# Attention scores from one 512-column product, its two halves added on the way out of PSUM

## The chip, the cores and the metric

The kernel runs on one core of a Trainium2 chip. The metric is the device time of one execution in microseconds (us). TensorE (PE in the profile) multiplies matrices, VectorE (DVE) and ScalarE (ACT) work elementwise, GpSimd (POOL) here issues DMAs and clears memory, SyncE (SP) issues most weight loads from HBM.

## The reference

A trunk of 4 layers over 256 tokens of width 2048, with 256 memory tokens. Layers 0 and 3 use multi-head latent attention (16 heads), layer 1 sparse attention (32 heads, the top 64 keys of a query), layer 2 sliding-window attention (32 heads, with sinks). Every layer also attends to the memory with 4 heads of width 256, gates, projects out and adds to the residual:

```
s = (einsum(qn, k_nope) + einsum(qr, k_rope)) * scale      # latent
s = einsum(qb, kg) * 64**-0.5 + bias                       # sparse, window
s = einsum(mq, mk) * 256**-0.5                             # memory
p = softmax(where(mask, s, -1e30));  o = p @ v
y = concat([self_out, mem_out]) * silu(gate);  x = x + y @ w_out[i]
```

All arithmetic is fp32.

## The kernel before

To get near fp32 precision from TensorE's faster fp32r format, the kernel keeps an operand as two fp32r parts: an exact part and a remainder (`split`, lines 67 to 69: ScalarE copies and rounds, L60, VectorE subtracts, L69). A product of two such operands is three products: exact by exact, exact by remainder, remainder by exact. All big projections are made so: `rows_by` (L265 to L267, three products of 512 columns for each 128 features) and `columns_by` (L285, one product whose 512 moving columns are the exact part and the remainder side by side, and L289, one of 256 columns). In `columns_by` the two halves of a PSUM bank hold two partial sums, which are added when the bank is read out (`total`, `head_parts`).

Weights come from HBM into a ring of 5 tiles `wr`; `parts_of` splits each 128x512 piece into `wh` and `wl` (rings of 3). So TensorE is fed by one L60 and one L69 for every 1536 columns or so.

The layers' work is split into six parts (two of memory heads, four of self heads). Each part has a projection, an attention and an output projection `w_out`. The instructions of all of them are put in order by the framework's planner, which simulates the engines with modelled durations; so a part's attention is threaded between the next part's projection products on TensorE. Each engine then executes its queue strictly in the planned order.

The scores of a head are made for two blocks of 128 queries, b = 0 and b = 1, in `score(b)`. Block 0 sees 128 keys, block 1 sees 256. In block 0 the keys' exact part and remainder (128 columns each) already are the moving columns of one 256-column product, and `masked_softmax` adds the second half with the bias (L527) before the fused add-and-minimum (L529, a `tensor_tensor_reduce`, followed by a read of its accumulator). In block 1, exact part and remainder are two products of 256 columns into the same 256 columns of PSUM, so L529 needs no addition before it. The memory heads (`memory_attend`, L577) make six products of 256 columns for each block, take the maximum (L588) and the exponential (L592) straight from PSUM. In the sparse layer the bias of a block is first added to the selection (`bs`, L962).

Small work tiles of these steps rotate through tags: `e` (4 buffers: `u`, `bs`, `e`, `th`), `mp` (4 PSUM banks).

Of the kernel before, what the change touches and what calls it, by code (L numbers as in the profile page):

```python
# [8 lines left out]
F32 = mybir.dt.float32  # L9
F32R = mybir.dt.float32r  # L10
I32 = mybir.dt.int32
AF = mybir.ActivationFunctionType
OP = mybir.AluOpType
AX = mybir.AxisListType

P = 128
S = 256
# [4 lines left out]
BIG = 3e38  # L22
# [9 lines left out]
def kernel(ctx: ExitStack, tc: tile.TileContext, a: dict, out: bass.AP,  # L32
                             kinds=(0, 1, 2, 0)):
    nc = tc.nc
# [4 lines left out]
    wk = ctx.enter_context(tc.tile_pool(name="wk", bufs=1))  # L39
# [9 lines left out]
    def small(name, n, dt=F32, bufs=None):  # L49
        return wk.tile([P, n], dt, name=name, tag=f"s{n}" if bufs is None else name,  # L50
                       bufs=bufs or 6)
# [7 lines left out]
    def copy_act(o, i, scale=1.0):  # L59
        inst = nc.scalar.activation(o, i, AF.Copy, scale=scale)  # L60
        if pinned:
            tc.keep_in_program_order(inst)
# [245 lines left out]
    class Norm:  # L308
# [37 lines left out]
        def finish(self):  # L346
            s2 = small("xs2", 2)
            nc.vector.tensor_reduce(s2, self.ss.rearrange("p (t c) -> p t c", t=2), AX.X, OP.add)
            self.rstd = small("xr", 2, bufs=3)
            rsqrt_mean(self.rstd, s2, D)  # L350
            self.eighth = small("x8", 2, bufs=3)
            nc.vector.tensor_scalar(self.eighth, self.rstd, 0.125, None, op0=OP.mult)
            half = small("xh", 2)
            nc.vector.tensor_scalar(half, self.rstd, 0.5, None, op0=OP.mult)
            self.half = wk.tile([P, S], F32, name="half", tag="half", bufs=1)
            spread(self.half, half)
# [158 lines left out]
    def masked_softmax(score, bias, scale=None, nsk=None):  # L515

        es = []
        mn, sm = small("mn", 2), small("sm", 2)  # L520
        for b in range(2):
            n = (b + 1) * P
            sp = score(b)
            u = wk.tile([P, S], F32, name="u", tag="e", bufs=4)
            bi = bias(b, n)
            if b == 0:
                nc.vector.tensor_add(u[:, :n], sp[:, n:2 * n], bi)  # L527
                bi = u[:, :n]
            nc.vector.tensor_tensor_reduce(u[:, :n], sp[:, :n], bi, -1.0,  # L529
                                           nsk if nsk is not None else BIG,  # L530
                                           op0=OP.add, op1=OP.min, accum_out=mn[:, b:b + 1])
            e = wk.tile([P, S], F32, name="e", tag="e", bufs=4) if nsk is None else u
            if scale is None:
                nc.scalar.activation(e[:, :n], u[:, :n], AF.Exp, bias=mn[:, b:b + 1], scale=-1.0,
                                     accum_out=sm[:, b:b + 1])
            else:
                ms = small("ms", 2)
                nc.vector.tensor_mul(ms[:, :1], mn[:, b:b + 1], scale[0][:, b:b + 1])
                nc.scalar.activation(e[:, :n], u[:, :n], AF.Exp, bias=ms[:, :1],
                                     scale=scale[1][:, b:b + 1], accum_out=sm[:, b:b + 1])  # L540
            es.append(e)
        r = small("rc", 2)
        if nsk is not None:
            d = small("sd", 2)
            nc.vector.tensor_scalar(d, mn, nsk, None, op0=OP.subtract)
            e2 = small("se", 2)
            nc.scalar.activation(e2, d, AF.Exp)
            s3 = small("sa", 2)
            nc.vector.tensor_add(s3, sm, e2)
            nc.vector.reciprocal(r, s3)  # L550
        else:
            nc.vector.reciprocal(r, sm)
        for b in range(2):
            normalized(es[b], r[:, b:b + 1], (b + 1) * P)
        return weights_T(es, [(0, 0), (1, 0), (1, 1)])
# [20 lines left out]
    def memory_attend(nm, kT, v, qT, gT):  # L576
        y = act.tile([P, 2, 4, S], F32R, name="y", tag="y", bufs=2)  # L577
        for h in range(2):
            es = []
            mn, sm = small("mn", 2), small("sm", 2)  # L580
            for b in range(2):
                sp = misc("msp")
                qs = slice(b * P, (b + 1) * P)
                seq = [(qT[h][:, u, k, qs], kT[h][:, v_, k, :])
                       for k in range(2) for u, v_ in ((0, 0), (0, 1), (1, 0))]
                for n_, (l, r_) in enumerate(seq):
                    nc.tensor.matmul(sp[:, :S], l, r_, start=n_ == 0, stop=n_ == len(seq) - 1)
                nc.vector.tensor_reduce(mn[:, b:b + 1], sp[:, :S], AX.X, OP.max, negate=True)  # L588
                ms = small("ms", 2)
                nc.vector.tensor_mul(ms[:, :1], mn[:, b:b + 1], nm.col("rstd", b))  # L590
                e = wk.tile([P, S], F32, name="e", tag="e", bufs=4)
                nc.scalar.activation(e, sp[:, :S], AF.Exp, bias=ms[:, :1], scale=nm.col("rstd", b),  # L592
                                     accum_out=sm[:, b:b + 1])
                es.append(e)
            r = small("rc", 2)
            nc.vector.reciprocal(r, sm)
            for b in range(2):
                normalized(es[b], r[:, b:b + 1], S)
            tp = weights_T(es, [(0, 0), (1, 0), (0, 1), (1, 1)])
            pH, pL = (wk.tile([P, 768], F32R, name="pT", tag="pT", bufs=PT)[:, :512] for z in range(2))  # L600
            split(pH, pL, tp)
            o = misc("mo")
            for j in range(2):
                c = (2 * h + j) * P
                seq = [(v[z][:, t, c:c + P], p_[:, t * S:(t + 1) * S])
                       for t in range(2) for z, p_ in ((0, pH), (0, pL), (1, pH))]
                for n_, (l, r_) in enumerate(seq):
                    nc.tensor.matmul(o[:, j * S:(j + 1) * S], l, r_, start=n_ == 0, stop=n_ == 5)
            gated(y, o, gT, 2 * h)
        return y  # L610
# [13 lines left out]
    class Latent:  # L624
# [102 lines left out]
        def attend(self, qn, qr, kn, v, gT):  # L727
            y = act.tile([P, 2, 4, S], F32R, name="y", tag="y", bufs=2)
            for h in range(4):
                def score(b):  # L730
                    sp = misc("sp")
                    qs = slice(b * P, (b + 1) * P)
                    q, k, z = qn[h // 2], kn[h // 2], h % 2
                    if b == 0:
                        seq = [(q[:, 0, z, qs], k[:, :, z, :P]), (q[:, 1, z, qs], k[:, :, z, :P]),
                               (qr[:, h, qs], self.kr[:, :, :P])]
                    else:
                        seq = [(q[:, 0, z, qs], k[:, 0, z, :]), (q[:, 0, z, qs], k[:, 1, z, :]),
                               (q[:, 1, z, qs], k[:, 0, z, :]),
                               (qr[:, h, qs], self.kr[:, 0, :]), (qr[:, h, qs], self.kr[:, 1, :])]  # L740
                    for n_, (l, r_) in enumerate(seq):
                        nc.tensor.matmul(sp[:, :S], l, r_, start=n_ == 0, stop=n_ == len(seq) - 1)
                    return sp
                tp = masked_softmax(score, lambda b, n: caus[:, S - n:], self.scale)
                pT = wk.tile([P, 768], F32R, name="pT", tag="pT", bufs=PT)
                pT = pT[:, :S], pT[:, S:2 * S], tmp("pf")[:, :P]
                split(pT[0], pT[1], tp[:, :S])
                copy_act(pT[2], tp[:, S:S + P])
                if h % 2 == 0:
                    o = misc("o")  # L750
                attend(o[:, (h % 2) * S:(h % 2 + 1) * S],
                       [z[:, h * P:(h + 1) * P] for z in v], pT)
                if h % 2 == 1:
                    gated(y, o, gT, h - 1)
            return y


    class Grouped:
# [182 lines left out]
        def attend(self, g, q, bm, gT):  # L941
# [3 lines left out]
            for h in (0, 2, 1, 3, 4, 6, 5, 7):  # L945
                def score(b):
                    sp = misc("sp")
                    qb = q[h // 4][:, h % 4, b * P:(b + 1) * P]
                    if b == 0:
                        nc.tensor.matmul(sp[:, :S], qb, self.k[:, g, :, :P], start=True, stop=True)  # L950
                    else:
                        for v in range(2):
                            nc.tensor.matmul(sp[:, :S], qb, self.k[:, g, v, :],
                                             start=v == 0, stop=v == 1)
                    return sp

                def bias(b, n):
# [171 lines left out]
    nm = Norm(0)  # L1129
# [3 lines left out]
    for i in range(depth):  # L1133
# [33 lines left out]
        else:  # L1167
            w_out(*pending, True)
            nxt.finish()
            nm = nxt  # L1170
# [62 lines left out]
```

## Time and profile before

| what | value |
|---|---|
| median of 3 runs | 2577.34 us (2576.85 to 2578.38) |
| profiled execution, span from first to last instruction | 2575.1 us |
| TensorE matmul busy | 2564.1 us, 13986 products |
| TensorE weight load busy | 2208.4 us |
| VectorE busy | 1906.1 us |
| ScalarE busy | 1621.0 us |
| TensorE clock granted | 0.999 of full speed |

The profile gives the profiled execution by its span alone; the runs' times also hold what lies around the span, and their median is 2.2 us above it. Matmuls are pipelined, so the duration of one in the trace is longer than the distance to the next one's start: the spacing of starts tells TensorE's rate. Weight loads (PEld) overlap the products.

### The profile page before, as it was taken

The page shows a single profiled execution, that of the slowest core. Times are in us where ns is not written, and L with a number is a line of the kernel's source. Part 1 is how long each engine was busy: PE and PEld are TensorE (multiplying, and loading weights), DVE is VectorE, ACT ScalarE, POOL GpSimd, SP SyncE. Part 2 cuts the span into 40 slices and gives each one's busy share as a digit, 9 for nine tenths or more (in the row PEclk, how much of TensorE's full clock was granted, in tenths as well). Part 3 has the DMA queues.
Part 4 walks back from the last instruction along what each step waited for, and adds up shares of the span by engine and source line. Part 5 has one row for each costly group of instructions (what it writes and reads, how often), then busy time and mean ns, then how long its engine had stood idle before and what let it go on. Part 6 is the DMA issues. An engine that isn't in the chain of part 4 may idle for free. (4 is left out here: it accounts for less than half of the span.)

```text
span 2575.1 us, 41628 instructions
## 1 busy us (share of the span) xinstructions
PE 2564.1 (100%) x13986; PEld 2208.4 (86%) x13986; DVE 1906.1 (74%) x4179; ACT 1621.0 (63%) x3467; POOL 87.1 (3%) x159
## 2 busy tenths in 40 slices
PE   9999999999999999999999999999999999999998
PEld 7888898888888888888888888888889888888887
DVE  6666667677777786887778776787878767777776
ACT  6556556556656566667666666676766655665665
POOL 1000000000000000000000000000000000000000
PEclk9999999999999999999999999999999999999999
DMA  9888777666676667566656575555655877676664
GB/s 303 258 259 267 239 212 235 185 170 191 196 201 201 203 213 246 173 197 188 196 165 197 170 226 170 169 183 185 196 156 148 241 201 198 196 196 181 212 173 179
DMA packets 459416, 520.02 MB, mean 202 GB/s; under 512 B 69520, under 2 KB 353056, under 8 KB 457536
## 3 DMA queue, kind: packets, MB, share of 16 engines
q1 hardware_dynamic: 441744, 449.72, 58.3%
q0 software_dynamic: 16736, 66.65, 8.0%
q8 instruction: 110, 1.80, 0.3%
q14 instruction: 106, 0.87, 0.1%
q10 hardware_dynamic: 720, 0.98, 0.1%
HBM read 494.10 MB, written 35.75 MB: 206 GB/s over the span
## 5 line engine op out<-in xcount | busy, mean ns | idle before, releaser
L69 DVE TENSOR_TENSOR wl<-wr,wh 128x512 fp32r<-128x512 f32 (+2 forms) x1720 | 1159.4, 677 | 579.1 <-ACT wh L60 555.5
L60 ACT ACTIVATE wh<-wr 128x512 fp32r<-128x512 f32 (+2 forms) x1720 | 1064.9, 621 | 801.7 <-PE acc_g L285 166.9
L285 PE MATMUL acc_g<-xT,wh 128*128 128x512 f32 x1536 | 484.7, 396 | 0.0
L289 PEld LDWEIGHTS acc_g<-xT,wl 128*128 128x128 f32 x1536 | 284.6, 188 | 63.0
L289 PE MATMUL acc_g<-xT,wl 128*128 128x256 f32 x1536 | 304.6, 280 | 0.0
L266 PE MATMUL acc_wo<-wl,y 128*128 128x512 f32 x752 | 297.3, 395 | 0.3 <-DVE wl L69 0.3
L267 PE MATMUL acc_wo<-wh,y 128*128 128x512 f32 x752 | 292.4, 390 | 0.0
L285 PEld LDWEIGHTS acc_g<-xT,wh 128*128 128x128 f32 x1536 | 235.9, 189 | 1.3
L265 PE MATMUL acc_wo<-wh,y 128*128 128x512 f32 x752 | 234.9, 392 | 0.1
L266 PEld LDWEIGHTS acc_wo<-wl,y 128*128 128x128 f32 x752 | 141.3, 188 | 28.5 <-DVE wl L69 1.2
L267 PEld LDWEIGHTS acc_wo<-wh,y 128*128 128x128 f32 x752 | 141.4, 188 | 27.1
L265 PEld LDWEIGHTS acc_wo<-wh,y 128*128 128x128 f32 x752 | 139.3, 188 | 28.5 <-ACT y L60 1.0
L285 PE MATMUL acc_mk<-mT,wh 128*128 128x512 f32 x512 | 161.5, 396 | 0.4 <-ACT wh L60 0.4
L285 PE MATMUL acc_mq<-xT,wh 128*128 128x512 f32 x512 | 161.6, 396 | 0.0
L1146 DVE TENSOR_TENSOR x<-x,acc_wo 128x512 f32<-128x512 f32 x184 | 122.3, 682 | 4.0 <-PE acc_wo L267 3.6
L285 PE MATMUL acc_qn<-cT,wh 128*128 128x512 f32 x384 | 121.3, 397 | 0.0
L285 PE MATMUL acc_cq<-xT,wh 128*128 128x512 f32 x384 | 120.9, 396 | 0.0
L289 PEld LDWEIGHTS acc_mk<-mT,wl 128*128 128x128 f32 x512 | 96.1, 188 | 22.8 <-DVE wl L69 0.4
L289 PEld LDWEIGHTS acc_mq<-xT,wl 128*128 128x128 f32 x512 | 93.7, 188 | 19.6
L289 PE MATMUL acc_mq<-xT,wl 128*128 128x256 f32 x512 | 103.4, 282 | 0.0
L266 PE MATMUL acc_q<-wl,xT 128*128 128x512 f32 x256 | 101.4, 396 | 0.0
L289 PE MATMUL acc_mk<-mT,wl 128*128 128x256 f32 x512 | 101.1, 278 | 0.0
(335 smaller groups left out, 4349.5 us busy)
## 6 DMA issues: line engine op xcount, KB each, us to landing
wr<-in_w_out_dram SPq DMA_DIRECT2D x188, 512.0 KB, 3.7
wr<-in_w_in_a_dram SPq DMA_DIRECT2D x176, 512.0 KB, 4.0
wr<-in_w_mem_kv_dram SPq DMA_DIRECT2D x120, 512.0 KB, 4.5
wr<-in_w_in_b_dram SPq DMA_DIRECT2D x112, 512.0 KB, 3.5
wr<-in_w_in_c_dram SPq DMA_DIRECT2D x104, 512.0 KB, 3.5
wr<-in_w_uq_dram SPq DMA_DIRECT2D x192, 128.0 KB, 2.9
wr<-in_w_uq_dram SPq DMA_DIRECT2D x48, 256.0 KB, 3.8
tab<-flat POOLq DMA_DIRECT2D x8, 1536.0 KB, 9.1
```

The lines of the kernel that those rows point to most:

```text
L60: inst = nc.scalar.activation(o, i, AF.Copy, scale=scale)
L69: nc.vector.tensor_sub(lo, src, f32(hi))
L265: nc.tensor.matmul(acc[t][:, :n], xh, wh[:, :n], start=first, stop=False)
L266: nc.tensor.matmul(acc[t][:, :n], xh, wl[:, :n], start=False, stop=False)
L267: nc.tensor.matmul(acc[t][:, :n], xl, wh[:, :n], start=False, stop=last)
L285: nc.tensor.matmul(acc[j], wh[:, o:o + P], q[:, :, kt % 4, :], start=kt == 0, stop=False)
L289: nc.tensor.matmul(acc[j][:, 0, :], wl[:, o:o + P], q[:, 0, kt % 4, :], start=False, stop=kt == kts - 1)
L1146: nc.vector.tensor_add(xs, xs, acc[t])
```

## The change

For block 1 of a latent or grouped head the keys' exact part and remainder become the 512 moving columns of one product, as in block 0, and the halves are added by a `tensor_add` of 128x256 with the bias (L527's operation) before the fused operation. In the latent layers the same is done for the rotary part: five products become three. For the memory heads six products of 256 columns become four (512, 256, 512, 256). ScalarE copies the second half to `u`, the fused operation replaces L588's maximum and leaves the negated scores in `u`, and the exponential reads `u` from SBUF, with the scale `neg`, a new small tile (the negated `rstd`) made once for each layer.

```
+            self.neg = small("xn", 2, bufs=3)
+            nc.vector.tensor_scalar(self.neg, self.rstd, -1.0, None, op0=OP.mult)
...
-            if b == 0:
-                nc.vector.tensor_add(u[:, :n], sp[:, n:2 * n], bi)
-                bi = u[:, :n]
-            nc.vector.tensor_tensor_reduce(u[:, :n], sp[:, :n], bi, -1.0,
+            nc.vector.tensor_add(u[:, :n], sp[:, n:2 * n], bi)
+            nc.vector.tensor_tensor_reduce(u[:, :n], sp[:, :n], u[:, :n], -1.0,
...
-                seq = [(qT[h][:, u, k, qs], kT[h][:, v_, k, :])
-                       for k in range(2) for u, v_ in ((0, 0), (0, 1), (1, 0))]
-                for n_, (l, r_) in enumerate(seq):
-                    nc.tensor.matmul(sp[:, :S], l, r_, start=n_ == 0, stop=n_ == len(seq) - 1)
-                nc.vector.tensor_reduce(mn[:, b:b + 1], sp[:, :S], AX.X, OP.max, negate=True)
+                for k in range(2):
+                    nc.tensor.matmul(sp, qT[h][:, 0, k, qs], kT[h][:, :, k, :], start=k == 0, stop=False)
+                    nc.tensor.matmul(sp[:, :S], qT[h][:, 1, k, qs], kT[h][:, 0, k, :], start=False, stop=k == 1)
+                u = wk.tile([P, S], F32, name="u", tag="e", bufs=4)
+                copy_act(u, sp[:, S:])
+                nc.vector.tensor_tensor_reduce(u, sp[:, :S], u, -1.0, BIG,
+                                               op0=OP.add, op1=OP.min, accum_out=mn[:, b:b + 1])
...
-                nc.scalar.activation(e, sp[:, :S], AF.Exp, bias=ms[:, :1], scale=nm.col("rstd", b),
+                nc.scalar.activation(e, u, AF.Exp, bias=ms[:, :1], scale=nm.col("neg", b),
...
-                        seq = [(q[:, 0, z, qs], k[:, 0, z, :]), (q[:, 0, z, qs], k[:, 1, z, :]),
-                               (q[:, 1, z, qs], k[:, 0, z, :]),
-                               (qr[:, h, qs], self.kr[:, 0, :]), (qr[:, h, qs], self.kr[:, 1, :])]
+                        seq = [(q[:, 0, z, qs], k[:, :, z, :]), (q[:, 1, z, qs], k[:, 0, z, :]),
+                               (qr[:, h, qs], self.kr)]
...
-                    if b == 0:
-                        nc.tensor.matmul(sp[:, :S], qb, self.k[:, g, :, :P], start=True, stop=True)
-                    else:
-                        for v in range(2):
-                            nc.tensor.matmul(sp[:, :S], qb, self.k[:, g, v, :],
-                                             start=v == 0, stop=v == 1)
+                    n = (b + 1) * P
+                    nc.tensor.matmul(sp[:, :2 * n], qb, self.k[:, g, :, :n], start=True, stop=True)
```

## Rows read from the trace of the kernel before

**Rows 1.** The page: the span and the busy time of each engine.

```profile
span 2575.1 us, 41628 instructions
PE 2564.1 (100%) x13986; PEld 2208.4 (86%) x13986; DVE 1906.1 (74%) x4179; ACT 1621.0 (63%) x3467; POOL 87.1 (3%) x159
```

**Rows 2.** Waits of PE, first and last of four: us, times, longest.

```profile
PE wu L102 <- DVE ones L98: 1.1, 1, 1.1
...
PE acc_wo L266 <- DVE wl L69: 0.3, 2, 0.2
```

**Rows 3.** Busy time by window: PE, PEld, DVE, ACT, POOL, clock, DMA.

```profile
960.00:1480.00 520.00, 519.78 (x2832) 446.05 (x2832) 411.02 (x965) 349.19 (x787) 16.68 (x24) 1.00 0.62 192
1080.00:1100.00 20.00, 20.00 (x109) 17.20 (x108) 19.55 (x59) 12.33 (x29) 0.76 (x1) 1.00 0.49 155
1160.00:1180.00 20.00, 20.00 (x100) 16.65 (x99) 14.66 (x39) 13.86 (x33) 0.00 (x0) 1.00 0.52 159
```

**Rows 4.** Groups by form on PE: the score products that the diff touches.

```profile
L742 PE MATMUL sp<-kn,qn 128*128 128x256 f32 x160 | 28.5, 288 | 0.0
L587 PE MATMUL msp<-mkr,mqT 128*128 128x256 f32 x192 | 28.1, 284 | 0.0
...
L953 PE MATMUL sp<-kd,qS 128*128 128x256 f32 x128 | 25.6, 282 | 0.0
```

**Rows 5.** Timeline of PE, 473 to 477: start, us, instructions merged.

```profile
473.52 0.88 PE L587 MATMUL msp<-mkr,mqT 128*128 128x256 f32 x6
474.24 0.40 PE L289 MATMUL acc_mq<-xT,wl 128*128 128x256 f32 x2
474.48 0.63 PE L285 MATMUL acc_mq<-xT,wh 128*128 128x512 f32 x2
...
475.17 0.63 PE L285 MATMUL acc_mq<-xT,wh 128*128 128x512 f32 x2
...
476.57 0.63 PE L285 MATMUL acc_mq<-xT,wh 128*128 128x512 f32 x2
```

**Rows 6.** Timeline of PE, 1439 to 1441: six products of contiguous columns.

```profile
1439.10 0.39 PE L265 MATMUL acc_wo<-wh,y 128*128 128x512 f32 x1
...
1440.46 0.86 PE L979 MATMUL o<-pT,vz 128*128 128x512 f32 x3
```

**Rows 7.** Timeline of PE, 565 to 567: three latent score products.

```profile
565.74 0.52 PE L742 MATMUL sp<-kr,qrT 128*128 128x256 f32 x3
566.10 0.40 PE L289 MATMUL acc_g<-xT,wl 128*128 128x256 f32 x2
```

**Rows 8.** Groups by form on DVE and ACT: busy, mean ns, idle before.

```profile
L60 ACT ACTIVATE z<-acc_g 128x256 f32<-128x256 f32 x96 | 35.2, 369 | 0.3
...
L592 ACT ACTIVATE e<-msp,ms,xr 128x256 f32<-128x256 f32 x32 | 17.8, 557 | 13.2 <-DVE ms L590 13.0
L534 ACT ACTIVATE u<-u,mn 128x256 f32<-128x256 f32 x32 | 15.9, 497 | 0.9 <-DVE mn L529 0.9
L529 DVE DVE_READ_ACCUMULATOR2_ANT mn<- 128x1 f32 x192 | 15.8, 82 | 0.0
L529 DVE CUSTOM_DVE_ANT_0 u<-sp,caus 128x256 f32<-128x256 f32 x32 | 13.3, 417 | 0.0
L588 DVE TENSOR_REDUCE mn<-msp 128x1 f32<-128x256 f32 x32 | 13.0, 419 | 4.1 <-PE msp L587 3.7
L304 DVE TENSOR_TENSOR zl<-acc_kn,kn 128x256 f32<-128x256 f32 x32 | 12.2, 415 | 0.1
L352 DVE TENSOR_SCALAR x<-xr 128x2 f32<-128x2 f32 x4 | 0.7, 168 | 0.1
```

**Rows 9.** Waits of DVE: the longest in total.

```profile
DVE wl L69 <- ACT wh L60: 555.5, 967, 2.7
```

**Rows 10.** Timeline, 1441 to 1443: a weight load that waits for DVE.

```profile
1441.58 0.68 DVE L69 TENSOR_TENSOR wl<-wr,wh 128x512 fp32r<-128x512 f32 x1
...
1442.31 0.19 PEld L266 LDWEIGHTS acc_wo<-wl,y 128*128 128x128 f32 x1 [0.59 <-DVE wl L69]
```

**Rows 11.** Timeline, 2566 to 2567: the last product of the kernel.

```profile
2566.42 0.28 PE L1013 MATMUL acc_wo<-wk,y 128*128 128x256 f32 x1
```

More of the change, by code (lines that the diff above doesn't have):

```diff
@@ L737, in score @@
                     else:
-                        seq = [(q[:, 0, z, qs], k[:, 0, z, :]), (q[:, 0, z, qs], k[:, 1, z, :]),
-                               (q[:, 1, z, qs], k[:, 0, z, :]),
-                               (qr[:, h, qs], self.kr[:, 0, :]), (qr[:, h, qs], self.kr[:, 1, :])]
+                        seq = [(q[:, 0, z, qs], k[:, :, z, :]), (q[:, 1, z, qs], k[:, 0, z, :]),
+                               (qr[:, h, qs], self.kr)]
                     for n_, (l, r_) in enumerate(seq):
-                        nc.tensor.matmul(sp[:, :S], l, r_, start=n_ == 0, stop=n_ == len(seq) - 1)
+                        n = r_.shape[-1] * (r_.shape[1] if len(r_.shape) == 3 else 1)
+                        nc.tensor.matmul(sp[:, :n], l, r_, start=n_ == 0, stop=n_ == 2)
                     return sp
```

## The prediction

> **What bounds the kernel now.** I read the page first, then the waits of TensorE, the busy time by window, the groups by form, and last the timeline around the score products.
>
> The page says that TensorE is busy for 2564.1 of 2575.1 us, VectorE for 1906.1 and ScalarE for 1621.0 [rows 1]. A busy TensorE is no proof, since a product's bar outlasts the start of the next one. Two more views make it one. TensorE's own waits come to 2.4 us over four entries, the first 1.1 us at the very start [rows 2]. And the spacing of starts is regular: six products of 256 columns start 0.72 us before what follows them, 0.12 us each [rows 5], three latent ones 0.36 us before, again 0.12 [rows 7]. The loop of `columns_by`, two products of 512 and two of 256 columns, has a period of (476.57 - 474.48) / 3 = 0.697 us [rows 5]. Six products of 512 contiguous columns take 1440.46 - 1439.10 = 1.36 us, 0.227 each [rows 6]. So 512 columns cost nearly what twice 256 cost: **TensorE runs at the rate of its columns, from the first microseconds to the last product at 2566.42** [rows 11]. The 8.4 us from that product's end to the end of the span (2575.1 - 2566.7) are the final norm and the output, which the diff doesn't touch.
>
> VectorE and ScalarE are cover. In layer 1, the widest of the touched stretches, VectorE is busy for 411 of 520 us while TensorE is busy for 519.8 [rows 3]. Even where VectorE is busy for 19.55 of 20 us, TensorE misses nothing [rows 3]. VectorE's longest wait is for ScalarE's `wh`, 555.5 us in 967 pieces [rows 9]: it mostly stands ready for the next weight tile.
>
> **The change part by part.**
>
> *Products.* Columns first, since they set the rate. Memory: 6 x 256 = 1536 before, 512 + 256 + 512 + 256 = 1536 after. Latent, block 1: 5 x 256 = 1280 before, 512 + 256 + 512 = 1280 after. Grouped, block 1: 512 before and after. Not one column goes away. What goes is instructions: 2 for each of 32 memory blocks (the 192 products of L587 at six a block), 2 for each of 32 latent heads (L742's 160 at five), 1 for each of 64 grouped heads (L953's 128 at two) [rows 4]: 192 products and 192 weight loads of 13986.
>
> What is each worth? For a memory block, six products at 0.72 become the loop's mix of two 512 and two 256, 0.697: -0.023 us, x 32 = -0.7 us [rows 5]. For a latent head, five at 0.12 = 0.60 become half the loop's period, 0.349, plus one of contiguous columns, 0.227, together 0.576: -0.024 x 32 = -0.8 us [rows 5 to 7]. For a grouped head, 0.24 becomes 0.227: -0.013 x 64 = -0.8 us [rows 5, 6] (I take L953's spacing from L587's, same shape). Sum -2.3 us, 12 ns for each product removed. The timeline is rounded to 0.01 us, so for a group the error is about as large as the gain: the bounds are 0 and twice this, -4.6 us. I take -2.
>
> *A rule against this price.* The Trainium skill, TensorE: Matmul & The Clock Gate, section "Back-to-back issue gap", gives a stream of load-and-product pairs as about 81 ns a product at 128 columns and 131 ns at 512. By a straight line between them (an estimate from that page) 256 columns are 98 ns, a merge saves 2 x 98 - 131 = 65 ns, and 192 merges save 12.5 us. This case's trace doesn't agree: 512 columns are 227 ns apart here, not 131 [rows 6]. I go by the trace; the mechanism is the first rival.
>
> *VectorE.* Added: 96 additions of 128x256 with one operand in PSUM (32 latent, 64 grouped heads), at L304's 415 ns: 39.8 us. For the 32 memory blocks, the fused operation at 417 and its accumulator read at 82 replace the maximum at 419: 80 ns each, 2.6 us. `neg`: 4 operations like the one at 168 ns, 0.7 us. Sum 43 us, 1.7% of the span [rows 8].
>
> *ScalarE.* Added: 32 copies from PSUM at 369 ns, 11.8 us; the exponential reads SBUF, 497 (L534, same size) for 557: -1.9 us. Sum +10 us [rows 8].
>
> I cost both at nothing. The cover is TensorE's queue of projection products: VectorE has 669 us without work (2575.1 - 1906.1), and in a busy attention window of 20 us, three heads' blocks would add 3 x 0.415 = 1.2 us to 14.66 [rows 3]. If all that cover were gone, the price would be 43 us. Behind each added operation on VectorE's queue stand the next `wl` and the next head's operations; a late `wl` is what would reach TensorE. ScalarE's +10 us stands against 954 us without work.
>
> *Where cover is thin.* At 1442.31 a weight load of `w_out` waits for a `wl` that VectorE, busy with the sparse layer's last heads and the gate, started late [rows 10]; the trace has a like place in layer 2. There, one addition of 0.415 us ahead of the `wl` may go straight to TensorE: I add 2 x 0.4 = 0.8 us.
>
> *Buffers.* The longer second half is in a PSUM bank that was allotted whole before. In the memory heads the bank now comes free when the fused operation has read it, before the exponential and not after; a head takes four `e` buffers instead of two, so that the next head's `e` waits for the transposes of this one. Between bounds of nothing and one exponential (0.557 us) for each of the 8 memory parts, 4.5 us, I take nothing: those stages also have TensorE's projections to run. No DMA is added or moved.
>
> **Sum.** -2.0 + 0.8 = -1.2 us: span 2573.9. The runs' median lies 2.2 us above the profiled span (2577.34 - 2575.1), so I forecast **2576.1 us: no difference that can be measured.** A measurement of this kernel can tell about 0.2%, 5.2 us, from no change. The likeliest case's own range: the product term from 0 to -4.6, the thin places and buffers from 0 to +5, so 2572.7 to 2582.4.
>
> **Rivals.**
>
> 1. *The removed weight loads pay (faster).* If a product's spacing were set by its weight load, a merged product would cost 0.12 us and not 0.227, and 192 merges would save up to 192 x 0.12 = 23 us: 2554 us. For it: a weight load's bar is long against 0.12 us, and loads are busy for 86% of the span [rows 1]. Against: the spacing of 512 columns, 0.227, is nearly twice that of 256, so columns and not loads set it. It decides from 27 ns a merge (5.2 / 192), more than double my price. Chance 0.05. By the page of the Trainium skill named above the time would be 12.5 us less, about 2565 us.
>
> 2. *VectorE comes late (slower).* The additions stand in the planned order ahead of `wl` splits; where several heads' blocks meet a gate's and an output projection's VectorE work, TensorE waits for `wl` as it does at 1442.31 (0.59 us [rows 10]). If it happens once for each of the 24 attention parts, at 0.4 to 0.6 us, it costs 10 to 14 us, less 2 from the products: some 2586 us. It decides from about 7 us of VectorE's 43 reaching TensorE, one sixth. For it: the existing place, and that the planner lays out a new order by modelled durations. Against: the window in which VectorE has 0.45 us to spare of 20 and TensorE still loses nothing [rows 3]. Chance 0.16.
>
> 3. *The change doesn't save TensorE work at all.* The gain per merge is 0 and all else is hidden: 2577 to 2578 us. It has the same verdict as my forecast, with which it shares 0.79.
>
> **How the numbers follow.** Within 0.2%: 0.79 (forecast and rival 3); slower 0.16 (rival 2); faster 0.05 (rival 1). The likeliest case's range runs to 2582.4 above; to leave out no more than 2 in 10 I go a little into the slower rival, to 2584; below I keep its end, 2572.7.
>
> **What would show it.** In the profile after: 192 fewer products and loads on TensorE (13794 each); VectorE's busy time up by about 43 us to 1949 and ScalarE's by 10; `L527`'s operation in a 128x256 form near 415 ns, 96 of them; the 512-column score products followed by the next start after 0.227 to 0.235 us; TensorE's waits still a few us in sum. I would be wrong if TensorE's waits for `wl` or `y` grew past 7 us (rival 2), or if the merged products were followed after less than 0.21 us (rival 1).

## The result, and the profile after

The changed kernel takes 2600.8 us (median of four runs, 2600.3 to 2601.83), the kernel before, on the same chip, 2577.49: a ratio of 1.0091 (95% interval 1.0079 to 1.0103), or **23.3 us slower**. I had forecast 2576.1, and the time lies above the range of 2572.7 to 2584. The span of the profiled execution grew by as much, from 2575.1 to 2598.5 us.

The page of the kernel after, its span and the busy times of its engines, stands against [rows 1]:

```profile
span 2598.5 us, 41435 instructions
...
PE 2572.9 (99%) x13794; PEld 2193.3 (84%) x13794; DVE 1938.9 (75%) x4311; ACT 1632.8 (63%) x3499; POOL 86.5 (3%) x159
```

The 192 products and weight loads are gone as forecast, and yet TensorE is busy for longer, by 8.8 us: a product whose successor comes late has a longer bar, so part of a loss hides in "busy". TensorE is now without a bar for 25.6 us (2598.5 - 2572.9), before for 11.0. Its waits, six of the ten entries (us, times, longest), against [rows 2]:

```profile
PE acc_wo L265 <- ACT y L60: 5.3, 5, 1.2
PE acc_wo L265 <- ACT wh L60: 4.2, 7, 1.0
PE o L977 <- DVE pT L69: 1.5, 3, 0.5
PE sp L952 <- DVE qS L473: 1.4, 2, 0.7
PE acc_wo L266 <- DVE wl L69: 1.1, 3, 0.5
PE wu L102 <- DVE ones L98: 1.1, 1, 1.1
```

All ten come to 16.7 us, where before they came to 2.4. Most of it is in the output projection (`acc_wo`), and what is late is `y` and `wh`, less `wl`.

The layers divide the loss. The first product of `acc_kv` opens layer 1, its last product stands near the start of layer 2 and the last of `acc_kva` near the start of layer 3. First and last starts are in the tile views, this of the kernel before (count: durations in ns, first and last start):

```profile
L265 PE MATMUL acc_kva<-wh,xT x64: 289/294/378, 363.3 to 1986.2; 128*128 128x288 f32 x64
...
L265 PE MATMUL acc_kv<-wh,xT x64: 389/389/478, 957.3 to 1513.3; 128*128 128x512 f32 x64
```

and this of the kernel after:

```profile
L265 PE MATMUL acc_kva<-wh,xT x64: 290/294/378, 362.8 to 2008.5; 128*128 128x288 f32 x64
...
L265 PE MATMUL acc_kv<-wh,xT x64: 389/389/478, 956.3 to 1525.1; 128*128 128x512 f32 x64
```

Layer 1 starts 1.0 us earlier than before, layer 2's mark is 11.8 us later, layer 3's 22.3. So the two layers of grouped heads lose all of it, 12.8 and 10.5 us. The latent layers, with half as many additions and as many merged products as the grouped ones, lose next to nothing. In the table below the stretches go from first product to first product of these projections.

### The profile page after: what moved, and what is told of

The parts are those of the page before. It is cut to its first block, busy times and chain, and to the rows that moved or that the text cites. A ratio compares the mean times of both kernels' runs of the same rounds, so it can differ in the third digit from the quotient of the medians.

```text
span 2598.5 us, 41435 instructions
## 1 busy us (share of the span) xinstructions
PE 2572.9 (99%) x13794; PEld 2193.3 (84%) x13794; DVE 1938.9 (75%) x4311; ACT 1632.8 (63%) x3499; POOL 86.5 (3%) x159
## 5 line engine op out<-in xcount | busy, mean ns | idle before, releaser
L289 PEld LDWEIGHTS acc_mk<-mT,wl 128*128 128x128 f32 x512 | 96.1, 188 | 22.8 <-DVE wl L69 0.4
```

The lines of the kernel that those rows point to most:

```text
L289: nc.tensor.matmul(acc[j][:, 0, :], wl[:, o:o + P], q[:, 0, kt % 4, :], start=False, stop=kt == kts - 1)
```

## The experiments

Grouped heads are those of layers 1 and 2, 32 each. "Layer 1" and "layer 2" in the table are the length of that layer's stretch against the kernel before, in us, from one profiled execution each. A ratio is against the kernel before on the same chip, whose median lay between 2577.25 and 2577.59 us. The last two columns are explained under "What the traces show together".

```
kernel                        median   ratio (95% interval)     layer 1  layer 2   splits 1   splits 2
before                        2577.49                                               0 0 0 0    0 0 0 0
after                         2600.8   1.0091 (1.0079, 1.0103)   +12.9    +10.5     0 4 4 4    0 4 4 4
e1_grouped_only               2601.0   1.0092 (1.0076, 1.0109)   +12.3    +11.4     0 4 4 4    0 4 4 4
e2_all_but_grouped            2579.52  1.0009 (0.9999, 1.0018)    -0.2     +1.7     0 0 0 0    0 0 0 0
e3_merged_no_add              2576.88  0.9998 (0.9989, 1.0008)    -0.2      0.0     0 0 0 0    0 0 0 0
e4_load_only                  2597.9   1.0081 (1.0066, 1.0096)   +10.0    +10.0     0 4 4 4    0 0 4 0
e5_chain_only                 2581.6   1.0018 (1.0008, 1.0027)    +3.8     +0.3     0 2 2 2    0 0 0 0
e6_load_in_gate               2586.61  1.0038 (1.0025, 1.0051)    +9.0     +0.5     0 2 2 2    0 0 0 0
e7_load_in_wout               2613.49  1.0139 (1.0124, 1.0154)   +17.5    +19.5     0 2 4 0    0 2 4 2
e8_add_elsewhere              2599.74  1.0088 (1.0073, 1.0103)   +20.0     +2.1     0 4 4 4    0 2 2 2
e9_bias_own_buffer            2591.93  1.0057 (1.0040, 1.0073)    +3.3    +10.4     0 2 2 2    0 4 4 4
e10_elsewhere_own_buffer      2600.46  1.0093 (1.0078, 1.0108)   +20.0     +2.2     0 4 4 4    0 2 2 2
e11_wout_relief               2593.79  1.0064 (1.0049, 1.0079)   +11.2     +6.8     0 4 2 4    0 4 2 2
e12_half_the_heads            2594.23  1.0067 (1.0052, 1.0082)   +11.6     +5.3     0 4 4 4    0 2 2 2
e13_gate_own_buffer           2592.93  1.0060 (1.0045, 1.0075)   +12.9     +1.3     0 4 4 4    0 0 0 0
e15_load_own_buffer           2587.12  1.0037 (1.0024, 1.0050)    -0.8    +11.0     0 0 0 0    0 0 4 0
e16_both_remedies             2583.71  1.0024 (1.0015, 1.0033)    +4.0     +2.1     0 2 2 2    0 2 2 2
e17_before_own_buffer         2576.26  0.9996 (0.9986, 1.0005)    -1.0      0.0     0 0 0 0    0 0 0 0
e18_both_buffers              2582.93  1.0022 (1.0013, 1.0032)    +3.9     +1.3     0 2 2 2    0 0 0 0
e19_before_both_buffers       2576.11  0.9996 (0.9986, 1.0006)    -1.0     -0.7     0 0 0 0    0 0 0 0
```

**Which part.** The change was cut in three: e1 is the kernel before with the grouped heads' merge and addition alone, e2 the change without these, and e3 has the grouped merge but no addition.

```
e1, in before:  if b == 0 or scale is None:     # scale is None: grouped heads; with e3's product
                    nc.vector.tensor_add(u[:, :n], sp[:, n:2 * n], bi)
                    bi = u[:, :n]
e3, in before:  n = (b + 1) * P
                nc.tensor.matmul(sp[:, :2 * n], qb, self.k[:, g, :, :n], start=True, stop=True)
```

> The kernel before with the change in the 64 grouped heads alone (merged product of 512 columns and the addition in block 1). Theory A (VectorE's added operations come between the weight splits where an output projection, a gate and heads meet, and TensorE waits): nearly all of the change's +23 us, so 2596 to 2603 us. Theory B (the whole plan shifts; the loss is spread over all layers and edits): a part only, 2582 to 2592. Theory C (the loss comes from the memory or latent heads): about 2577.

> The changed kernel with the grouped heads as before: latent and memory heads stay changed. Theory A: 2575 to 2580 us, TensorE's idle and late starts as before. Theory B: 2584 to 2592. Theory C: about 2600.

> The kernel before with the grouped heads' merged product of 512 columns, but without the addition: block 1 leaves the remainder's half of the scores out. VectorE's work is that of the kernel before. Theory A (VectorE's added operation is the cost): 2575 to 2578 us. A rival, that the wide product, or the plan made for it, is the cost: 2590 to 2600.

e1 loses all that the change loses; e2 loses some 2 us, which the measurement can't tell from nothing. e3 gives no difference either: its stretches sum to -0.3 us for 64 merged products. So the loss is not in the wide product but comes with the 64 additions on VectorE.

**Time on VectorE, or the head's chain?** The first theory: the additions' own time reaches TensorE where VectorE has none left, in the output projections. Its rival: a head's chain of steps has become longer. e4 adds to the kernel before one unrelated VectorE addition ahead of each grouped head's fused operation; e5 adds a step on ScalarE to the chain, and nothing on VectorE; e6 and e7 put eight additions a part into the gate's or the output projection's products.

```
e4:  junk = wk.tile([P, S], mybir.dt.bfloat16, name="jk", tag="jk", bufs=1)
     nc.vector.tensor_add(junk, bi, bi)                  # grouped heads, b == 1
e5:  copy_act(u, sp[:, :S]); sp = u                      # grouped heads, b == 1
e6:  if extra and k2 == 0: nc.vector.tensor_add(<jk>, wr[:, :S], wr[:, :S])   # in columns_by, gate
e7:  if extra and k == 0:  nc.vector.tensor_add(<jk>, wr[:, :S], wr[:, :S])   # in rows_by, w_out
```

> The kernel before with one VectorE addition of 128x256 more for each grouped head (64), from the bias tile into a small tile that nobody reads: the load without the merged product and without a longer chain from scores to exponential. If VectorE's load alone costs: 2592 to 2603 us. If the longer chain in the head (product, addition, fused operation, exponential) costs: 2576 to 2581.

> The kernel before, with a copy of block 1's scores from PSUM to SBUF on ScalarE ahead of the fused operation in the 64 grouped heads: the chain of a head gets longer by 0.37 us and a semaphore, VectorE's work stays. Theory A (VectorE's load in the output projections of the grouped layers is the cost): 2575 to 2581 us. If the chain's length costs: 2592 to 2603.

> The kernel before with 64 unrelated VectorE additions of 128x256 in all, eight in each grouped part's gate projection, a stage in which VectorE was busy for some 0.83 of the time. If only the output projection's stretch binds (there VectorE was busy throughout): 2577 to 2583 us. If VectorE binds over the whole cycle of a part: 2592 to 2603, as with the load in the heads.

> The kernel before with 64 unrelated VectorE additions of 128x256 in all, eight in each grouped part's output projection, where VectorE was busy throughout. If that stretch binds: 64 x 0.42 = 27 us, of which some can be given back by heads that move to other stretches: 2592 to 2606 us. If the cost lies in the heads' own order: 2577 to 2583.

The unrelated operation costs 20.6 us (2597.9 against 2577.33), nearly what the addition costs; the chain's ScalarE step costs 4. So a VectorE operation at this place is enough. Where the work stands decides its price: eight additions a part cost 0.5 us in the gate of layer 2 and 19.5 in its output projections. In layer 1 the gate's cost 9.0, which the first theory did not foresee. e5, e6 and e7 lie outside both of their ranges: e5 by 0.6 us, e6 between the two, e7 7.5 us above the upper one.

**Which resource.** e8 keeps the changed kernel and gives the grouped block 1's addition to ScalarE (copy) and GpSimd (addition). e11 takes work off VectorE in the output projections: the grouped layers' residual addition is left out and ScalarE copies the product instead. e12 has the change in every second grouped head.

```
e8:   copy_act(u[:, :n], sp[:, n:2 * n])
      nc.gpsimd.tensor_add(u[:, :n], u[:, :n], bi)
e11:  copy_act(xs, acc[t])                       # for: nc.vector.tensor_add(xs, xs, acc[t])
e12:  if b == 0 or h % 2: (one product of 2 * n columns, and the addition)
```

> The changed kernel, but in block 1 of the grouped heads ScalarE copies the second half out of PSUM and GpSimd adds the bias in SBUF; VectorE is left with the work of the kernel before there. If VectorE's load is the cost: 2574 to 2582 us, in spite of a longer chain. If the wide product, the longer chain or the new order is the cost: 2592 to 2605.

> The changed kernel with VectorE relieved in the grouped layers' output projections: the residual addition there is left out, ScalarE copies the product out of PSUM instead (5.5 us less of VectorE's work for each part, 12 parts). If VectorE binds in that stretch: 2574 to 2582 us, the whole loss is given back. If the heads' own chain or the new order costs: 2592 to 2602.

> The kernel before with the merged product and the addition in every second grouped head only (32 of 64). If VectorE stood at its limit already, the loss is in proportion: 10 to 14 us, 2587 to 2592. If there was some slack to use up first, the first half is nearly free: 2577 to 2583.

e8 cures layer 2 (+2.1 us) and makes layer 1 worse (+20.0). On GpSimd the addition takes nearly twice VectorE's 420 ns and waits for ScalarE's copy, in the groups by form of e8 (busy us, mean ns, idle before):

```profile
L530 POOL TENSOR_TENSOR u<-u,bm 128x256 f32<-128x256 f32 x32 | 25.7, 802 | 358.2 <-ACT u L60 228.0 <-DVE u L532 107.0 <-DVE x L1148 23.2
L530 POOL TENSOR_TENSOR u<-u,bs 128x256 f32<-128x256 f32 x32 | 24.8, 776 | 276.4 <-ACT u L60 136.8 <-DVE wl L69 96.2 <-PE acc_g L285 25.4
```

e11 gives back 7 us and not the whole, and half the heads (e12) cost half in layer 2 but nearly all in layer 1. A price per operation, the first theory, allows neither: e12 lies above both of its ranges, e8 and e11 in the upper ones. The theory falls in this form.

**The ring of `e` buffers.** The second theory: `u`, `bs`, `e` and the gate's `th` share four buffers. A longer step inside a head holds its buffers longer, and the planner can only place the next users later. e9 takes the sparse layer's bias `bs` out of the ring of the changed kernel, e13 the window layer's `th`; e10 is e8 with `bs` out, e15 is e4 with `bs` out, e16 has `bs` out and e8's addition in layer 2, e18 has `bs` and `th` out. e17 and e19 are the kernel before with `bs`, and with both, out.

```
e9:   two.append(spare(1, "bs"))          # a buffer of its own, 512 wide, for both blocks
      bs = two[-1][:, b * S:]             # for: bs = wk.tile([P, S], F32, name="bs", tag="e", bufs=4)
e13:  if now[0] == 2:                     # the window layer
          if j == 0: two = spare(1, "th")
          th = two[:, j * S:(j + 1) * S]  # for: th = wk.tile([P, S], F32, name="th", tag="e", bufs=4)
```

> The changed kernel, with the sparse layer's bias tile in a buffer of its own, out of the ring of four that scores and weights share. VectorE's work is that of the changed kernel. If VectorE's load costs in both grouped layers: within 4 us of the changed kernel (2597 to 2603), layer 1 still some 10 us longer than before. If in the sparse layer the ring of four sets the heads' pace: layer 1 gives back most of its 13 us, 2586 to 2592.

> The same buffer for the kernel that adds block 1's halves with ScalarE and GpSimd, in which layer 2 stood 2 us above before and layer 1 20 us. If the ring of four, held longer by GpSimd's 0.78 us addition, was what cost there: 2578 to 2586 us. If the longer chain through GpSimd itself, or GpSimd's queue, costs: 2592 to 2602.

> The changed kernel with the tanh tiles of the window layer's gates in a buffer of their own, out of the ring of four; VectorE's work as in the changed kernel. If VectorE's load is the cost in layer 2: layer 2 stays 9 to 11 us longer than before, 2598 to 2602 us. If the ring is the cost there as well: layer 2 gives back most of its 10.5, 2590 to 2594.

> The kernel before with the unrelated VectorE operation in the grouped heads and the sparse layer's bias tile in a buffer of its own. Layer 2 is as in the load-only run, 10 us longer. If in layer 1 the ring was what turned the load into a loss: layer 1 at most 4 us longer than before, 2588 to 2593. If load alone costs there too: 9 to 11 us, 2595 to 2599.

> The changed kernel with the bias tile's own buffer in the sparse layer, and in the window layer block 1's halves added by ScalarE and GpSimd. If each remedy meets its layer's cause: 23.4 us less 9.6 less 8.4 above before, 2581 to 2585 us. If the causes are shared between the layers, it comes out otherwise: 2588 or more.

> The kernel before with the sparse layer's bias tile in a buffer of its own. If the ring set nothing there (TensorE loses 5 us in all): 2575 to 2579 us. If it already held back the sparse layer: 2570 to 2575.

> The changed kernel, all 43 us of VectorE's additions in place, with the sparse layer's bias tile and the window layer's tanh tiles out of the ring of four. If the ring is the cause in both layers: 23.4 us less 9.6 less 9.2 above before, 2580 to 2584 us. If VectorE's load still costs on its own: 2588 or more.

> The kernel before with the same two buffers. If the ring was just wide enough there: 2574 to 2578 us. If it held back the grouped layers already: 2568 to 2574.

With the same operations on VectorE, one tile moved to another buffer gives back 9.6 us in layer 1 (e9) and 9.2 in layer 2 (e13), and both together take the loss from 23.4 to 6.5 us by the stretches (e18). In e15 the unrelated operations cost layer 1 nothing once `bs` is out (2587.12 us in all, just under the range). The same buffers in the kernel before change nothing that can be measured (e17, e19), so they are no gain that any kernel would have: they take away what the additions brought. The miss is e10: freeing `bs` does nothing for e8's layer 1. No version of the change beats the kernel before.

**What the traces show together.** This reading came after the runs, and no expectation speaks of it. A grouped part's cycle on TensorE is an output projection (`acc_wo`), the next part's queries (`acc_q`) and its gate (`acc_g`); the heads of a part run under these. Before its heads can run, a part needs four `qS` splits on VectorE (L471 before, L473 after), each 0.69 us, with as many roundings on ScalarE. One such cycle in layer 2, the busy time of tile `qS` by window (length; PE, PEld, DVE, ACT, each with its count), in the kernel before:

```profile
1689.40:1713.70 24.30, 1.12 (x6) 0.91 (x6) 0.00 (x0) 0.00 (x0) 1.00 0.56 174
1713.70:1738.80 25.10, 1.80 (x9) 1.25 (x9) 0.00 (x0) 0.00 (x0) 1.00 0.52 165
1738.80:1766.10 27.30, 1.79 (x9) 1.47 (x9) 2.75 (x4) 2.36 (x4) 1.00 0.62 196
```

in the kernel after:

```profile
1698.50:1729.20 30.70, 1.77 (x6) 1.05 (x6) 2.67 (x4) 2.25 (x4) 1.00 0.54 170
1729.20:1754.30 25.10, 1.78 (x6) 0.90 (x6) 0.00 (x0) 0.00 (x0) 1.00 0.52 167
1754.30:1779.20 24.90, 1.11 (x4) 0.68 (x4) 0.00 (x0) 0.00 (x0) 1.00 0.54 171
```

and in e13, with the same additions and `th` out of the ring:

```profile
1704.40:1728.80 24.40, 1.10 (x4) 0.68 (x4) 0.00 (x0) 0.00 (x0) 1.00 0.53 168
1728.80:1754.90 26.10, 1.71 (x6) 0.97 (x6) 0.00 (x0) 0.00 (x0) 1.00 0.54 166
1754.90:1780.90 26.00, 1.26 (x4) 0.68 (x4) 2.58 (x4) 2.15 (x4) 1.00 0.60 195
```

Before and in e13 the four splits run under the gate (x4 in the third line); after the change they have slid into the next stretch, under the output projection (x4 in the first). The cycle is 76.7 us before, 80.7 after, 76.5 in e13. All engines over the output projection, first before, then after (PE, PEld, DVE, ACT, POOL):

```profile
1689.40:1713.70 24.30, 24.30 (x116) 20.21 (x115) 21.47 (x52) 16.31 (x39) 0.00 (x0) 1.00 0.56 174
```

```profile
1698.50:1729.20 30.70, 28.50 (x133) 22.05 (x132) 26.44 (x62) 20.00 (x45) 0.00 (x0) 1.00 0.54 170
```

VectorE has 5 us more to do there, more than half of it the four splits, and TensorE is idle for 2.2 us even by its long bars. The timeline of the kernel after shows one such place (start, us, engine, instruction, in brackets what it waited for):

```profile
1707.17 0.69 DVE L473 TENSOR_TENSOR qS<-tr,qS 64x512 fp32r<-64x512 f32 x1
...
1707.90 0.69 DVE L983 TENSOR_TENSOR yt<-o,gT 128x512 f32<-128x512 f32 x1
1708.00 0.40 PE L267 MATMUL acc_wo<-wh,y 128*128 128x512 f32 x1
1708.43 0.63 ACT L60 ACTIVATE wh<-wr 128x512 fp32r<-128x512 f32 x1 [2.34 <-PE acc_wo L267]
...
1708.97 0.61 ACT L60 ACTIVATE y<-yt 128x512 fp32r<-128x512 f32 x1
...
1709.64 0.50 PE L265 MATMUL acc_wo<-wh,y 128*128 128x512 f32 x1 [1.24 <-ACT y L60]
```

VectorE splits a `qS` for the next part, and only then makes `yt`, the last piece that this output projection needs; ScalarE rounds a `wh` before it takes up `y`; TensorE stands for 1.24 us.

That order is not new. In the kernel before, the last split stands ahead of the same `yt`, but both run before the output projection starts:

```profile
1762.82 0.69 DVE L471 TENSOR_TENSOR qS<-tr,qS 64x512 fp32r<-64x512 f32 x1
...
1764.87 0.69 DVE L985 TENSOR_TENSOR yt<-o,gT 128x512 f32<-128x512 f32 x1
...
1766.14 0.63 PE L265 MATMUL acc_wo<-wh,y 128*128 128x512 f32 x2
```

So VectorE's order at this place did not change. What moved is where the end of a part's heads stands against the projections. The last `yt` started 1.3 us before the first product of its output projection (1764.87 against 1766.14), and after the change 9.4 us behind it (1707.90 against 1698.50). The splits go with the end of the heads and tell how late it is.

The columns "splits 1" and "splits 2" of the table count, for layers 1 and 2, the `qS` splits that start in each of the first four output projections of a layer, a projection counted from its first product behind the gate's last one. A layer with none loses at most 1.7 us (e2), one with two in each of three projections 2.1 to 9.0 (e8, e6), one with four in each of three 10.0 to 20.0 (e4, e8). Over the 144 output projections of all kernels but e7 and e11, which change this stretch themselves: with no split in it 22.4 to 25.5 us (median 24.3, 85 of them), with two 25.2 to 27.1 (25.2, 27), with four 28.3 to 32.4 (30.3, 32). In the second to fourth projection of each layer of these kernels, 108 in all, the last split starts 0.7 to 3.8 us ahead of the last `yt`, and that `yt` starts at most 1.7 us behind the start of its projection where no split stands in it, 3.7 to 5.4 behind where two do, and 7.7 to 12.9 where four do. Part of this is work moved out of the gate's stretch, as the cycle shows: the net price is 4.0 us in the cycle shown, where four splits slid, and 0.9 where two did (e8's cycle in layer 2, 25.2 + 26.9 + 25.5 = 77.6 us). The two layers have six output projections with four: 6 x 4.0 = 24 us (an estimate from that one cycle), for a loss of 23.4.

The columns also fit the runs that the theories missed. Half the heads (e12) bring all four splits over in layer 1, but only two in layer 2. e8 and e10 have four in layer 1, with `bs` in or out of the ring, and two in layer 2. In e11, which gave back a part, three of the six stretches kept four.

What stays open: that TensorE loses by heads that end late was read from these traces, since no run moved the last `yt` or the splits alone. Why e8 and e10 keep four splits in layer 1 was not tried; their last `yt` starts 9.3 to 12.9 us behind there, and their loss, 20.0, is more than three cycles' 12. In layer 2 of e4 and e15 one projection alone has four, and yet the loss is 10 to 11 us. That stretch of e4 holds more than the slide (timeline of TensorE, then a window with the clock before its last two numbers):

```profile
1784.71 0.47 PE L265 MATMUL acc_wo<-wh,y 128*128 128x512 f32 x1 [2.04 <-DVE z L296]
1786.15 0.80 PE L266 MATMUL acc_wo<-wl,y 128*128 128x512 f32 x1 [0.97 <-DVE wl L69]
...
1787.17 0.63 PE L266 MATMUL acc_wo<-wl,y 128*128 128x512 f32 x1
1787.60 0.63 PE L267 MATMUL acc_wo<-wh,y 128*128 128x512 f32 x1
```

```profile
1785.70:1789.10 3.40, 2.95 (x7) 2.37 (x8) 2.99 (x11) 1.66 (x4) 0.00 (x0) 0.50 0.32 123
```

TensorE stood 2.04 us for a late `z`, VectorE's reading of the gate's PSUM bank (`total`); then its granted clock was 0.50 for 3.4 us, the lower of its two levels (1.2 and 2.4 GHz), and products of 512 columns started 0.43 us apart, against 0.23 at the upper level. That is some 1.6 us of the loss (an estimate: 3.4 us less eight products at 0.227). e15's profile shows the same at this place. e6's and e10's have one such fall of 3.4 us in layer 1, and e7's has three, 17.0 us in all, so that some 8 us of e7's loss are the clock's (estimated alike). The price of a slide thus depends on more than the count. e11 put its copies onto ScalarE, busy there for 22.8 of 29.7 us, so it does not tell VectorE's share from the order of its queue.

## Why the prediction was wrong

**Products: the count right, the gain too small to measure.** 13794 of them, as forecast, and the added operations on VectorE take 418 to 422 ns, where I had 415, as the groups by form of the kernel after show:

```profile
L528 DVE TENSOR_TENSOR u<-sp,bs 128x256 f32<-128x256 f32 x32 | 13.5, 422 | 0.9
...
L528 DVE TENSOR_TENSOR u<-sp,caus 128x256 f32<-128x256 f32 x32 | 13.4, 419 | 0.0
L528 DVE TENSOR_TENSOR u<-sp,bm 128x256 f32<-128x256 f32 x32 | 13.4, 418 | 0.0
```

For the grouped heads I had -0.8 us; e3 gives -0.3, less than executions of one kernel differ. By the section "Back-to-back issue gap" of the Trainium skill's page TensorE: Matmul & The Clock Gate, named in the prediction, 64 merges at the estimated 65 ns would have given 4.2 us, and e3 does not agree. For the memory and latent heads I had -1.5; e2, with their additions, gives +2.3 by its stretches, of which layers 0 and 1 are shorter (-0.6 and -0.2). The first rival, loads that pay 23 us, has no support: the products are fewer and e3's time is unchanged.

**VectorE's sum: right work, smaller busy time.** I expected +43 us, the page says +32.8. Operations of the queue overlap at their ends: e4's 64 additions of 0.42 us make 26.9 us in sum, and its busy time grew by 20.6 (1926.7 - 1906.1). ScalarE's +11.8 is near the +10, in part by luck: I took the memory heads' new exponential at 497 ns from L534, whose scale is a constant. With its scale from a column it takes 597 (L594, last section), so that it added 1.3 us where I had taken off 1.9.

**"I cost both at nothing": this step failed.** It argued from VectorE's 669 us without work and from the window 1080 to 1100, where VectorE was busy for 19.55 of 20 us and TensorE lost nothing [rows 3]. But the first grouped score product of that trace starts at 1114.0, as the tile view of `sp` shows:

```profile
L950 PE MATMUL sp<-kd,qS x64: 278/362/365, 1114.0 to 1907.4; 128*128 128x256 f32 x64
```

The window holds no grouped head, so it could not show what a head with a longer step does. The term that I put at nothing measured 20.6 us with 64 VectorE operations alone (e4) and 23.7 with the merge and the additions of the grouped heads (e1, 2601.0 against 2577.33). Idle time summed over the span was no cover, because by the traces what reached TensorE was less the added 0.42 us than what it delayed: the heads of a part ended some 10 us later against the projections (9.4 us behind the start of their output projection, where it had been 1.3 before it), so that TensorE waited there for `y` and `wh`. The cover itself was ample by the sum: a `wl` of 0.68 us [rows 10] feeds six products of 512 columns, 1.36 us [rows 6], some 3000 columns and not the 1536 that the section on the kernel before gives.

**"Buffers": looked at the wrong heads.** I asked after the ring `e` in the memory heads only, and took nothing. It was in the grouped heads, where `u`, `bs` and `th` compete, that it set the place of later work (e9, e13, e18).

**"Where cover is thin", and the second rival.** The place was right, output projections that wait behind VectorE's queue [rows 10], and so was the sign; I gave the rival 0.16. Its price, 24 parts at 0.4 to 0.6 us, was of the wrong shape: the loss is six output projections at some 4 us each, and what is late is `y` and `wh` as much as `wl`. The sign that I named, waits for `wl` or `y` past 7 us, comes to 6.4 in the two entries above; the view of waits alone, 16.7 us, shows less than the loss.

**What the change costs without this.** With both buffers in both kernels, 2582.93 - 2576.11 = 6.8 us. By the stretches of the profiled executions, whose spans differ by 7.9, 3.9 + 1.0 us are in layer 1, where two splits still slide, and 1.3 + 0.7 in layer 2, where none does. The trade is a bad one even then: e3 shows next to nothing saved on TensorE that could pay for the additions.

## What to carry to other kernels

Where a planner or a queue orders the work, an operation on an engine with spare time is not free until it is known which tiles it holds and what they will delay: list the users of each ring that the operation's tiles rotate through, in every kind of head, before it is costed at nothing. A window that is to prove cover must hold the very operations that the change touches. After a change, compare where the same small tile (here the four `qS` splits, or the last `yt`) runs against the start of the stage that needs it: a slide into the next stretch says more than busy shares.

## What the runs showed of the hardware

A merged product saves almost nothing here: 64 merges, each one product of 512 columns for two of 256, shortened the stretches by 0.3 us, some 5 ns each. The exponential of the memory heads has its scale from a column in both kernels, and was slower from SBUF (597 ns) than it had been from PSUM (557) [rows 8]. From SBUF, at the same size, exponentials took 497 to 505 ns with a constant scale (L534) and 587 to 597 with the scale from a column (L539, L594). GpSimd took 776 to 802 ns for the addition, both operands in SBUF, that VectorE does in 420. In e4 TensorE's granted clock was at the lower level for 3.4 us right after a wait of 2.04. The groups by form of the kernel after:

```profile
L594 ACT ACTIVATE e<-u,ms,xn 128x256 f32<-128x256 f32 x32 | 19.1, 597 | 8.8 <-DVE ms L592 8.8
L539 ACT ACTIVATE e<-u,ms,qsn 128x256 f32<-128x256 f32 x32 | 18.8, 587 | 0.0
...
L60 ACT ACTIVATE u<-msp 128x256 f32<-128x256 f32 x32 | 11.8, 369 | 5.6 <-PE msp L586 5.6
```
